# A decoder block with expert retrieval: row gathers through four buffers, tied to their blocks, and dense tiles normed one by one

## The chip, the cores and the metric

The kernel runs on one core of a Trainium2 chip. The metric is the device time in microseconds of one execution. TensorE (PE) multiplies matrices, VectorE (DVE), ScalarE (ACT) and GpSimd (POOL) work on tiles, and SyncE (SP) issues transfers. Each engine takes its instructions in the order in which they stand in its queue: an instruction that waits holds up all that stand behind it.

## The reference

A block of a decoder over 1024 tokens and 16 meta tokens (width 1024): a convolution branch and an RWKV-7 branch side by side, gated and mixed, then a channel mixer that looks up experts (PEER), then a norm. This study turns on the channel mixer and the norm:

```python
s = jnp.einsum('thcd,hcnd->thcn', q, sub_keys)          # 8 heads, 2 x 128 keys
...                                                     # top 16 of each, top 16 of the sums
e = (i1 * PEER_NKEYS + i2).reshape(TOK_BLOCK, PEER_HEADS * K)     # 128 experts per token
gate = jax.nn.softmax(best_s, axis=-1).reshape(TOK_BLOCK, PEER_HEADS * K)
u = expert_u[e]
act = jax.nn.gelu(jnp.einsum('td,ted->te', xb, u), approximate=False)
coef = (gate * act.astype(jnp.float32)).astype(xb.dtype)
return jnp.einsum('te,ted->td', coef, expert_v[e])
...
h = h + peer_ffn(rmsnorm(h, g_ffn[l]), ...)
return rmsnorm(h, g_final)[:, N_META:]
```

There are 16384 experts, 128 blocks of 128. Each expert has a row of 1024 in `expert_u` and one in `expert_v`.

## The kernel before

The 1024 tokens are eight tiles of 128, in two halves. The convolution, the recurrence, the mixing and the routing run for half 0 and then for half 1. The channel mixer is done in two ways at once.

**Three tiles (0, 1, 2) by gathering.** `gather_rows` is a generator. For each of 128 places `j` of a tile it takes a buffer `row` (128 x 2048, 8 KB per partition, `NROW` = 3 of them), issues on GpSimd an indirect DMA (L1005) that fetches for each token the rows u and v of its j-th expert from `euv`, 1 MB in all, multiplies on VectorE the u half with the token's input and sums (L1008, "the product"), takes Gelu and the gate on ScalarE (L1009, L1010), and adds the v half, scaled, to the tile's sum `yr` in PSUM (L1000, "the add"). A buffer is free again after the add. For tile 0 the input `xng` is read from SBUF, for tiles 1 and 2 it is first copied to PSUM (`xr`, L996). When a tile's 128 rows are done, `final` (L1035 on) norms it and stores it. `xng` has two buffers, which the input, the residual `y0` of tiles 1 and 2 and the norm's `sqf` share.

**Five tiles (4 to 7 and 3) densely.** `spread_gates` turns indices and gates into a dense matrix of gates per block of experts. `u_stage` multiplies all 512 tokens of half 1 with the u of one block (24 matmuls of 512 columns) and takes Gelu. For 68 of the 128 blocks (`PRE`) this happens ahead, and the result goes to memory and is read back as `g`. Tile 3's activations come from `gather_coefs`, which gathers u rows alone (L1027) in two runs, before and after place `NEARLY` = 62.

The dense stage is `dense`. It takes groups of `NB` = 4 blocks. For each block it gets the activations, multiplies them with the gates (L1134) and splits the result into a high and a low part, `c2` (L223 on ScalarE, L224 on GpSimd; the profile calls it `c`). Then, for each half `n` of the 1024 columns, it loads the v of the four blocks (`vraw`), splits them likewise (`vhi`, `vlo`), and for each of the five tiles runs 12 matmuls (four blocks, three each: `mm3`, L227 to L229) into one of four PSUM banks, which VectorE adds into the tile's sum (L1161; `hbuf`, `hr` in the profile). After each block it calls the generator for tiles 1 and 2: 8 rows at block 3, then 2 per block, the last at block 127.

In the last group ScalarE squares and sums each finished half of a dense tile (L1164). After the loop, the generator is run out (`for _ in rows`), `g_final` is loaded, the five tiles' sums are normed together (`rstd`: two tiny operations of VectorE, Ln, Exp and Square on ScalarE, two more on VectorE), and each tile is scaled by its factor and by `g_final` and stored. Tiles with even number in the list on VectorE, with odd number by ScalarE (L1174) and GpSimd (L1175).

**Order.** The order of every engine's queue is fixed when the program is built: a list scheduler walks through the instructions with estimated durations, and takes, for each engine, the ready instruction that comes first in the program. Buffers are given out by the same walk. `tc.issue_after(x)` adds that an instruction stands behind `x` on the same engine. It is used before the change for 14 gathers of tile 0 (`pace`). `tc.high_priority(offset=LATER)` puts the gathers of tiles 3 and 0 behind all other work of their stretch. Tile 0 runs beside the mixing, routing and spreading of half 1 and ends shortly after the dense stage has begun, at about 2315 us.

**Tiles of half 1.** Indices and gates of each half are `idx0`, `gate0`, `idx1` and `gate1` (128 x 512 each), made by `residual`. `hist` holds the last columns of the convolution's input from half 0 for half 1, and `carry` the recurrence's state between the halves and then the last output tile of the recurrence.

## Time and profile before

| | us |
|---|---|
| median of three runs | 3659.9 |
| lowest and highest | 3624.96, 3678.22 |
| the profiled execution | 3653.25 |
| its span, first to last instruction | 3651.5 |
| PE busy | 3282.5 (90%) |
| DVE busy | 2684.8 (74%) |
| POOL busy | 2280.4 (62%) |
| ACT busy | 1563.9 (43%) |
| mean granted clock of PE | 0.944 |
| moved by the DMA | 867.66 MB, 238 GB/s |

The profiled execution is one run. Its own time stands beside its span, and what lies around the span is under 2 us. A share of busy time is a mean over stages with different limits; the rows below go by stage. A PE matmul's duration in a row covers its pipeline, so matmuls overlap, and their pace is read from the distance of their starts.

### The profile page before, as it was taken

What the parts mean: (1) busy time and instruction counts of PE and PEld (TensorE: products, weight loads), DVE (VectorE), ACT (ScalarE), POOL (GpSimd) and SP (SyncE); (2) the same over time, 40 slices, a digit from 0 to 9 for tenths busy, and PEclk for the clock granted to TensorE, in tenths of its full rate; (3) what the DMA queues carried; (4) which work ended last, traced back from release to release, by engine and by line L of the source; (5) the groups of instructions that cost most, each with busy time, mean ns of one, the idle gap of its engine ahead of it and who ended that gap; (6) DMA issues with size and microseconds to landing.
All of it is one profiled execution on the core that took longest, in us unless ns stands there. A gap on an engine that the chain in (4) does not pass through costs nothing.

```text
span 3651.5 us, 49244 instructions
## 1 busy us (share of the span) xinstructions
PE 3282.5 (90%) x16175; PEld 2635.6 (72%) x16175; DVE 2684.8 (74%) x5108; ACT 1563.9 (43%) x3714; POOL 2280.4 (62%) x2123
## 2 busy tenths in 40 slices
PE   7999998888788998788899996899999998989994
PEld 7887776677566776676688885777777776777773
DVE  2566538969986775899999887666767666667777
ACT  5555443243444444433367774333333343333333
POOL 3442304535787655656888886676777766767774
PEclk9999979999998899999899998999999999999997
DMA  4321213333677676854699999888889888888987
GB/s 152 113 66 48 60 44 121 107 131 97 199 222 243 180 230 226 308 183 153 215 333 345 351 344 317 285 316 311 319 331 333 332 304 309 319 305 316 329 329 277
DMA packets 347381, 867.66 MB, mean 238 GB/s; under 512 B 53208, under 2 KB 132704, under 8 KB 293876
## 3 DMA queue, kind: packets, MB, share of 16 engines
q0 software_dynamic: 75328, 475.06, 36.0%
q1 hardware_dynamic: 182436, 328.77, 26.9%
q10 hardware_dynamic: 89360, 60.68, 5.4%
q8 instruction: 128, 2.10, 0.2%
q14 instruction: 129, 1.06, 0.1%
HBM read 777.48 MB, written 86.92 MB: 237 GB/s over the span
## 4 chain that ended last, share of the span: by engine, by line
PE 30%; DVE 20%; DMA 13%; issue 10%; POOL 8%; ACT 2%; POOLq 0%; ACTq 0%; DVEq 0%; SPq 0%
DMA row<-euv,idx 6%; PE zp L227 5%; PE zp L229 5%; PE zp L228 5%; PE py L227 3%; PE pg L1088 3%; PE py L228 3%; PE py L229 3%; POOL vlo L224 2%; DVE row L1008 2%; DMA gd<-gt 2%; DVE yr L1000 2%; DVE cy L348 2%; DMA vraw<-euv 2%; POOL row L1027 2%
## 5 line engine op out<-in xcount | busy, mean ns | idle before, releaser
L1005 POOL DMA_INDIRECT row<-euv,idx x384 | 411.2, 1071 | 319.6 <-DVE yr L1000 231.9
L1000 DVE SCALAR_TENSOR_TENSOR yr<-row,act,yr 128x1024 f32<-128x1024 f32 x384 | 493.2, 1284 | 153.9 <-ACT act L1010 151.6
L1008 DVE SCALAR_TENSOR_TENSOR row<-row,xr 128x1024 f32<-128x1024 f32 x256 | 311.5, 1217 | 164.4 <-DMA row<-euv,idx 157.5
L224 POOL TENSOR_TENSOR vlo<-vraw,vhi 128x512 fp32r<-128x512 f32 x256 | 330.8, 1303 | 156.7 <-ACT vhi L223 139.9
L224 POOL TENSOR_TENSOR ul<-ur,uh 128x512 fp32r<-128x512 f32 x256 | 340.3, 1336 | 38.6 <-ACT uh L223 32.2
L1009 ACT ACTIVATE act<-act 128x1 f32<-128x1 f32 x384 | 76.7, 200 | 644.2 <-DVE row L1008 635.3
L227 PE MATMUL py<-vhi,c 128*128 128x512 f32 x640 | 259.0, 409 | 75.8 <-DVE hbuf L1161 32.6
L227 PE MATMUL zp<-x,uh 128*128 128x512 f32 x784 | 315.5, 402 | 7.9 <-ACT g L1101 7.9
L229 PE MATMUL zp<-x,ul 128*128 128x512 f32 x784 | 314.4, 401 | 6.3 <-POOL ul L224 6.3
L228 PE MATMUL zp<-x,uh 128*128 128x512 f32 x784 | 314.4, 401 | 0.0
L229 PE MATMUL py<-vhi,c 128*128 128x512 f32 x640 | 255.6, 406 | 17.0 <-POOL c L224 16.7
L227 PE MATMUL zp<-vhi,c 128*128 128x512 f32 x640 | 251.4, 401 | 21.4 <-DVE hbuf L1161 15.2
L223 ACT ACTIVATE vhi<-vraw 128x512 fp32r<-128x512 f32 x256 | 159.9, 626 | 255.7 <-DMA vraw<-euv 129.4
L228 PE MATMUL py<-vlo,c 128*128 128x512 f32 x640 | 257.1, 402 | 0.4 <-POOL vlo L224 0.4
L228 PE MATMUL zp<-vlo,c 128*128 128x512 f32 x640 | 251.8, 398 | 0.0
L229 PE MATMUL zp<-vhi,c 128*128 128x512 f32 x640 | 249.3, 398 | 0.0
L348 DVE SCALAR_TENSOR_TENSOR cy<-u,vec,cy 128x512 f32<-128x512 f32 x240 | 243.4, 1014 | 5.4
L1008 DVE SCALAR_TENSOR_TENSOR row<-row,xng 128x1024 f32<-128x1024 f32 x128 | 217.4, 1700 | 14.3 <-DMA row<-euv,idx 14.3
L1029 DVE SCALAR_TENSOR_TENSOR row<-row,xng 128x1024 f32<-128x1024 f32 x128 | 184.5, 1447 | 57.4 <-DMA row<-euv,twice 57.1
L1027 POOL DMA_INDIRECT row<-euv,twice x128 | 152.7, 1193 | 111.7 <-DVE row L1029 73.0
L227 PEld LDWEIGHTS py<-vhi,c 128*128 128x128 f32 x640 | 124.3, 194 | 118.6 <-DVE hbuf L1161 43.3
L223 ACT ACTIVATE uh<-ur 128x512 fp32r<-128x512 f32 x256 | 159.3, 625 | 98.6 <-PE zp L228 51.0
(1666 smaller groups left out, 9267.7 us busy)
## 6 DMA issues: line engine op xcount, KB each, us to landing
vraw<-euv SPq DMA_DIRECT2D x256, 256.0 KB, 6.0
ur<-eut SPq DMA_DIRECT2D x256, 256.0 KB, 6.0
gd<-gt ACTq DMA_DIRECT2D x20, 1920.0 KB, 20.8
gblk<-gd SPq DMA_DIRECT2D x30, 1280.0 KB, 11.4
gs<-g SPq DMA_DIRECT2D x68, 256.0 KB, 7.1
g<-gs SPq DMA_DIRECT2D x68, 256.0 KB, 5.9
wbr<-w_in SPq DMA_DIRECT2D x64, 256.0 KB, 3.0
wqr<-w_q SPq DMA_DIRECT2D x64, 256.0 KB, 3.4
```

Of the source, the lines that this page charges most:

```text
L223: A.activation(hi, src, AF.Copy)
L224: return eng.tensor_sub(lo, src, hi.bitcast(F32))
L227: PE.matmul(ps, whi, xhi, start=first, stop=False)
L228: PE.matmul(ps, whi, xlo, start=False, stop=False)
L229: PE.matmul(ps, wlo, xhi, start=False, stop=last)
L348: V.scalar_tensor_tensor(y, u[:, j:j + 512], cw, y, op0=OP.mult, op1=OP.add)
L1000: V.scalar_tensor_tensor(y, row[:, 1], act[:, j:j + 1], y, op0=OP.mult, op1=OP.add)
L1005: G.indirect_dma_start(out=row.rearrange("p a d -> p (a d)"), out_offset=None, in_=a["euv"], in_offset=bass.IndirectOffsetOnAxis(ap=idx[0] ...
L1008: V.scalar_tensor_tensor(row[:, 0], row[:, 0], 1.0, xn, op0=OP.mult, op1=OP.mult, accum_out=aj)
L1027: G.indirect_dma_start(out=row, out_offset=None, in_=a["euv"].rearrange("e (k d) -> (e k) d", k=2), in_offset=bass.IndirectOffsetOnAxis(ap ...
L1029: V.scalar_tensor_tensor(row, row, 1.0, xn, op0=OP.mult, op1=OP.mult, accum_out=act[:, j:j + 1])
L1088: PE.matmul(pg[:, x], o2[:, x], o1[:, x], start=True, stop=True)
```

## The change

- `NROW` goes from 3 to 4: four row buffers for all gathers of whole rows and for the second run of `gather_coefs`. Its first run stays at three.
- Each gather of tiles 1 and 2 is put, in GpSimd's queue, behind the split of the current block's coefficients (`after[0]`).
- `xng` has one buffer instead of two. The input, the residual, the norm's result and `g_final` take turns in it.
- `idx1` and `gate1` are no tiles of their own any more: they are `hist` (made as wide as they need) and `carry`.
- The 256 rows of tiles 1 and 2 are dealt evenly to blocks 3 to 119: 8 at block 3, then `256 * (b + 1) // 120 - 256 * b // 120`, 2 or 3 per block. Blocks 120 to 127 have none. The generator is run out before the second half of the last group, `tables()` loads the table of Ln and Exp there, and `g_final` is loaded.
- Each dense tile is normed and stored right after its last add in the second half of the last group (`last`), with all multiplications on VectorE.

```diff
@@ -37,8 +37,9 @@
 DT = list(range(4, 8)) + list(range(NGT, 4))
 NG, NQ, GB, NB = WD // GT, 512 // GT, 4, 4
 PRE = [b for b in range(128) if b // 4 % 2 == 0 or b >= 120]
-NROW = 3
+NROW = 4
 NV2 = 6
+NROWS, LAST = (NGT - 1) * P, 120
 SOONER = 300
 PACE0 = 22
 NEARLY = 62
@@ -162,8 +163,8 @@
             h = hp.tile([P, 4, D], F32, name="hbuf1")
             hb1.append(h)
             hb.extend(h[:, t] for t in range(4))
-        idx.append(hp.tile([P, 4, P], I32, name=f"idx{hf}"))
-        gate.append(hp.tile([P, 4, P], F32, name=f"gate{hf}"))
+        idx.append(hist.bitcast(I32) if hf else hp.tile([P, 4, P], I32, name="idx0"))
+        gate.append(carry if hf else hp.tile([P, 4, P], F32, name="gate0"))
         if hf == 0:
             coef.append(hp.tile([P, P], F32, name="coef"))
 
@@ -171,7 +172,7 @@
 
         return pool(top, "hb0r")
     idx, gate, coef = [], [], []
-    hist = cp.tile([P, 4, NCONV - 1], F32, name="hist")
+    hist = cp.tile([P, 4, P], F32, name="hist")
     carry = cp.tile([P, 4, P], F32, name="carry")
     si = [0] * 4
     def tables():
@@ -978,13 +979,13 @@
         return x2
 
 
-    def gather_rows(gp, tiles, nrow, pace, yp, rp=None):
+    def gather_rows(gp, tiles, nrow, pace, yp, rp=None, after=()):
 
         for tt in tiles:
-            xn = gp.tile([P, D], F32, name="xng", bufs=2)
+            xn = gp.tile([P, D], F32, name="xng")
             G.dma_start(xn, xg[tt])
             act = gp.tile([P, P], F32, name="act")
-            y0 = gp.tile([P, D], F32, name="y0", tag="hr0" if rp is None else "xng", bufs=1 if rp is None else 2)
+            y0 = gp.tile([P, D], F32, name="y0", tag="hr0" if rp is None else "xng")
             G.dma_start(y0, hd[tt])
             y = hb[tt] = yp.tile([P, D], F32, name="yr")
             moves = [(y, y0)]
@@ -1001,7 +1002,7 @@
 
             for j in range(P):
                 row = gp.tile([P, 2, D], F32, name="row", bufs=nrow)
-                with tc.issue_after(pace[j]) if j in pace else ExitStack():
+                with tc.issue_after(after[0]) if after else tc.issue_after(pace[j]) if j in pace else ExitStack():
                     G.indirect_dma_start(out=row.rearrange("p a d -> p (a d)"), out_offset=None, in_=a["euv"],
                                          in_offset=bass.IndirectOffsetOnAxis(ap=idx[0][:, tt, j:j + 1], axis=0))
                 aj = act[:, j:j + 1]
@@ -1017,13 +1018,13 @@
 
     def gather_coefs(gp, tt, j0, j1):
 
-        xn = gp.tile([P, D], F32, name="xng", bufs=1 + (j1 == P))
+        xn = gp.tile([P, D], F32, name="xng")
         G.dma_start(xn, xg[tt])
         act = coef[0]
         twice = gp.tile([P, j1 - j0], I32, name="twice")
         V.tensor_single_scalar(twice, idx[0][:, tt, j0:j1], 1, op=OP.logical_shift_left)
         for j in range(j0, j1):
-            row = gp.tile([P, D], F32, name="row", bufs=NROW)
+            row = gp.tile([P, D], F32, name="row", bufs=NROW if j1 == P else 3)
             G.indirect_dma_start(out=row, out_offset=None, in_=a["euv"].rearrange("e (k d) -> (e k) d", k=2),
                                  in_offset=bass.IndirectOffsetOnAxis(ap=twice[:, j - j0:j - j0 + 1], axis=0))
             V.scalar_tensor_tensor(row, row, 1.0, xn, op0=OP.mult, op1=OP.mult, accum_out=act[:, j:j + 1])
@@ -1034,7 +1035,7 @@
     def final(sp, tt, nrow):
         y = hb[tt]
         ss = sp.tile([P, 1], F32, name="ssf")
-        q = sp.tile([P, D], F32, name="sqf", tag="xng", bufs=2)
+        q = sp.tile([P, D], F32, name="sqf", tag="xng")
         A.activation(q, y, AF.Square, accum_out=ss)
         r = rstd(sp, ss, 1, 1.0 / D, 1e-6, "rf")
         gq = sp.tile([P, 2, D], F32, name="gq", tag="row", bufs=nrow)[:, 0]
@@ -1104,7 +1105,8 @@
     def dense(es, x2, gp, hr, direct, gk1, vr, yp):
 
         cb = pool(es, "cb")
-        rows = gather_rows(gp, range(1, NGT), NROW, {}, yp, pool(es, "rp", 1, PSUM))
+        after = [None]
+        rows = gather_rows(gp, range(1, NGT), NROW, {}, yp, pool(es, "rp", 1, PSUM), after)
         vb = pool(es, "vb", 2, side="right")
         gk = [hr, gk1]
         yps = pool(es, "yps", 2, PSUM)
@@ -1116,6 +1118,14 @@
 
         gtile = None
         ss = cb.tile([P, 2, NDT], F32, name="ssd")
+        def last(t, tt):
+
+            V.tensor_add(ss[:, 0, t:t + 1], ss[:, 0, t:t + 1], ss[:, 1, t:t + 1])
+            r = rstd(cb, ss[:, 0, t:t + 1], 1, 1.0 / D, 1e-6, f"rd{t % 2}")
+            q = cb.tile([P, D], F32, name="yo", tag="c2", bufs=NB + 1)
+            V.scalar_tensor_tensor(q, hb[tt], r, gf, op0=OP.mult, op1=OP.mult)
+            (A if t % 2 else SY).dma_start(out[tt * P:(tt + 1) * P], q)
+
         for g0 in range(0, P, NB):
             blks = range(g0, g0 + NB)
             cs = []
@@ -1133,7 +1143,7 @@
                     act = u_stage(b, None, x2, bank())
                 V.tensor_mul(g1.rearrange("p (q t) -> p q t", q=NQ), act.rearrange("p (q t) -> p q t", q=NQ), gtile[:, :NQ, b % GB])
                 c2 = cb.tile([P, 2, WD], F32R, name="c2", bufs=NB + 1)
-                split(c2[:, 0, :512], c2[:, 1, :512], g1)
+                after[0] = split(c2[:, 0, :512], c2[:, 1, :512], g1).ins
                 split(c2[:, 0, 512:].rearrange("p (q t) -> p q t", t=GT), c2[:, 1, 512:].rearrange("p (q t) -> p q t", t=GT),
                       gtile[:, NQ:, b % GB])
                 cs.append(c2)
@@ -1141,7 +1151,7 @@
                     for tt in range(NGT, 4):
                         hb[tt] = gp.tile([P, D], F32, name="hr3", tag="hr0")
                         SY.dma_start(hb[tt], hd[tt])
-                for _ in range(0 if b < NB - 1 else 2 * NB if b == NB - 1 else 2):
+                for _ in range(0 if b < NB - 1 else NROWS * (b + 1) // LAST - (NROWS * b // LAST if b >= NB else 0)):
                     next(rows, None)
             for n in range(2):
                 ns = slice(512 * n, 512 * n + 512)
@@ -1153,6 +1163,12 @@
                     lo = vb.tile([P, 512], F32R, name="vlo", bufs=NV2)
                     split(hi, lo, raw)
                     vs.append((hi, lo))
+                if n and g0 == P - NB:
+                    for _ in rows:
+                        pass
+                    tables()
+                    gf = gp.tile([P, D], F32, name="gf", tag="xng")
+                    SY.dma_start(gf, a["g_fin"].to_broadcast([P, D]))
                 for t, tt in enumerate(DT):
                     tsl = slice(t * P, t * P + P)
                     ys = bank()
@@ -1162,20 +1178,8 @@
                     if g0 == P - NB:
                         q = gk[t % 2].tile([P, 512], F32, name="sq", tag="gblk")
                         A.activation(q, hb[tt][:, ns], AF.Square, accum_out=ss[:, n, t:t + 1])
-        for _ in rows:
-            pass
-        gf = cb.tile([P, D], F32, name="gf", tag="c2", bufs=NB + 1)
-        SY.dma_start(gf, a["g_fin"].to_broadcast([P, D]))
-        V.tensor_add(ss[:, 0], ss[:, 0], ss[:, 1])
-        r = rstd(cb, ss[:, 0], NDT, 1.0 / D, 1e-6, "rd")
-        for t, tt in enumerate(DT):
-            q = cb.tile([P, D], F32, name="yo", tag="c2", bufs=NB + 1)
-            if t % 2:
-                A.activation(hb[tt], hb[tt], AF.Copy, scale=r[:, t:t + 1])
-                G.tensor_mul(q, hb[tt], gf)
-            else:
-                V.scalar_tensor_tensor(q, hb[tt], r[:, t:t + 1], gf, op0=OP.mult, op1=OP.mult)
-            (A if t % 2 else SY).dma_start(out[tt * P:(tt + 1) * P], q)
+                        if n:
+                            last(t, tt)
 
     def convolution(hf, es, z, between):
         cv = pool(es, f"cc{hf}", side="right")
```

Left out of the diff are the two lines that read and write `hist`, which now name its first 30 columns.

## Rows read from the trace of the kernel before

**Rows 1.** Windows: stretch, length, busy us PE PEld DVE ACT POOL, clock, DMA share, GB/s
```profile
1850.00:2255.00 405.00, 376.86 (x2237) 329.31 (x2235) 353.45 (x639) 284.80 (x759) 333.16 (x303) 0.98 0.99 342
...
2255.00:3602.00 1347.00, 1252.18 (x5276) 1003.29 (x5276) 938.39 (x1227) 485.89 (x1238) 949.63 (x884) 0.97 0.87 316
...
3602.00:3652.00 50.00, 0.47 (x3) 0.04 (x1) 30.19 (x41) 16.08 (x36) 13.27 (x10) 0.53 0.67 249
```

**Rows 2.** Waits of PE, 2255 to 3602: total us, times, longest us
```profile
PE py L227 <- DVE hbuf L1161: 32.6, 16, 6.5
...
PE py L227 <- ACT c L223: 23.0, 13, 3.6
...
PE py L229 <- POOL c L224: 16.7, 11, 2.5
...
PE zp L227 <- DVE hbuf L1161: 15.2, 8, 4.8
```

**Rows 3.** Timeline of one stall: start us, us; in brackets idle before and releaser
```profile
3034.15 0.96 POOL L1005 DMA_INDIRECT row<-euv,idx  x1 [0.16 <-DMA vraw<-euv]
...
3044.76 1.22 DVE L1008 SCALAR_TENSOR_TENSOR row<-row,xr 128x1024 f32<-128x1024 f32 x1 [8.16 <-DMA row<-euv,idx]
...
3045.90 0.68 DVE L1161 TENSOR_TENSOR hbuf<-hbuf,py 128x512 f32<-128x512 f32 x1
...
3046.64 0.79 PE L227 MATMUL py<-vhi,c 128*128 128x512 f32 x1 [6.48 <-DVE hbuf L1161]
...
3047.23 0.63 PE L228 MATMUL py<-vlo,c 128*128 128x512 f32 x1
...
3051.50 0.63 PE L229 MATMUL py<-vhi,c 128*128 128x512 f32 x1
```

**Rows 4.** Waits of DVE and POOL, 2255 to 3602, same columns
```profile
DVE row L1008 <- DMA row<-euv,idx: 153.9, 95, 8.2
...
POOL row L1005 <- DVE yr L1000: 161.0, 75, 7.2
```

**Rows 5.** The gathers (L1005), 2330 to 3500: their starts, and landing
```profile
L1005 POOL DMA_INDIRECT row<-euv,idx x222: 935/961/1440, 2344.7 to 3495.1; - x111
...
DMA to landing us min/median/max: 5.4/8.1/13.0
```

**Rows 6.** Timeline of the end: last group's matmuls, the last tiles' norms
```profile
3593.15 0.39 PE L227 MATMUL zp<-vhi,c 128*128 128x512 f32 x1
...
3602.07 0.40 PE L229 MATMUL py<-vhi,c 128*128 128x512 f32 x1
...
3602.70 0.68 DVE L1161 TENSOR_TENSOR hr<-hr,py 128x512 f32<-128x512 f32 x1
...
3603.41 0.63 ACT L1164 ACTIVATE sq<-hr 128x512 f32<-128x512 f32 x1 [1.26 <-DVE hr L1161]
...
3640.22 1.29 DVE L1000 SCALAR_TENSOR_TENSOR yr<-row,act,yr 128x1024 f32<-128x1024 f32 x1 [0.60 <-ACT act L1010]
...
3641.54 1.02 ACT L1038 ACTIVATE sqf<-yr 128x1024 f32<-128x1024 f32 x1 [1.35 <-DVE yr L1000]
...
3642.67 1.28 ACT L201 ACT_TABLE_LOAD   x1
...
3647.66 0.33 SPq L1043 DMA_DIRECT2D out<-sqf  x1
```

**Rows 7.** Tile 1 to 2: timeline, then DMA issues (KB, us to landing)
```profile
3000.99 1.28 DVE L1042 SCALAR_TENSOR_TENSOR sqf<-yr,rfr,gq 128x1024 f32<-128x1024 f32 x1
...
3005.10 1.24 ACT L996 ACTIVATE xr<-xng 128x512 f32<-128x512 f32 x2 [0.62 <-DMA xng<-xg]
...
out<-sqf SPq DMA_DIRECT2D x2, 512.0 KB, 4.9
...
xng<-xg POOLq DMA_DIRECT2D x2, 512.0 KB, 8.2
...
y<-hd POOLq DMA_DIRECT2D x2, 512.0 KB, 8.1
```

More of the change, by code (lines that the diff above doesn't have):

```diff
@@ L332, in convolved @@
         else:
-            V.tensor_copy(u[:, :H], hist[:, ct])
+            V.tensor_copy(u[:, :H], hist[:, ct, :H])
         for t0, n, ps in zmain(hi, lo):
@@ L340, in convolved @@
         if off:
-            G.tensor_copy(hist[:, ct], u[:, 512:])
+            G.tensor_copy(hist[:, ct, :H], u[:, 512:])
         y = cv.tile([P, 512], F32, name="cy", bufs=4)
```

## The prediction

> **What bounds the kernel now.** I read the windows by stage first, then TensorE's waits in the dense stage, then one of its stalls in the timeline, then the last 50 us, and last the gathers and the DMA. The windows [rows 1] show a program that is TensorE's until 3602 us: in the 1347 us of the dense stage PE is busy 1252 us at a granted clock of 0.97, DVE 938 us, POOL 950 us. After that come 50 us in which PE does nothing and DVE, the busiest engine, works 30. So there are two places to gain: the tail, and what keeps the dense stage above its floor. The floor: two matmuls of the last group, 40 apart with both ends counted, start 3593.15 and 3602.07, so 39 steps of 0.229 us [rows 6]; 5280 matmuls (32 groups x 2 halves x 5 tiles x 4 blocks x 3, and 60 blocks x 24) take 1208 us at that pace. The stage takes 1347.
>
> What lies between is waiting. PE waits 47.8 us for VectorE's adds into the dense accumulators (32.6 + 15.2, 24 times), and 39.7 us for the coefficients (23.0 + 16.7) [rows 2]. A wait costs more than itself: at 3046.64 PE resumes after 6.48 us, and the matmuls from 3047.23 to 3051.50 start 0.43 us apart (10 steps), the lower of the two clock levels in pace, before the 0.229 returns [rows 3]. Twelve matmuls at 0.2 us more are 2.4 us, 37% on top of the gap. The same rows show why VectorE was late: its queue is in order, and a row's product (L1008) stood at its head for 8.16 us until the gather issued at 3034.15 had landed; the add that PE needed (L1161) came right behind it at 3045.90. Over the stage these products wait 153.9 us for their rows, 95 times, and GpSimd waits 161.0 us, 75 times, for a row buffer to come free (yr L1000) before it can issue a gather [rows 4], with the splits of the next weights queued behind.
>
> The gathers are near the limit of three buffers. 222 of them start between 2344.7 and 3495.1, one per 5.2 us, and land in 8.1 us (median) [rows 5]. A buffer is held from the issue to the end of the row's add: at least 8.1 + 1.2 (product) + 0.6 (two activations) + 1.3 (add) = 11.2 us [rows 3, 5, 6], and at one row per 5.2 us with three buffers at most 15.6. That is why rows are still to come when PE stops: the last add ends at 3641.5 [rows 6].
>
> **The change part by part.** All terms are set against the profiled execution, 3653.25 us (span 3651.5); the median of the three runs, 3659.9, is 6.7 above it.
>
> 1. The tail: the rows dealt to 120 blocks, dense tiles normed one by one. The last matmul ends 3602.47 and the span 3651.5, 49.0 us. With rows dealt so that the last belongs to block 119, two whole groups of four blocks follow, each about 10.5 us per block (1347 / 128), 84 us: the rows and the norm of tile 2 are done before PE is. Then what follows the last matmul is the last dense tile alone. Its add starts 0.23 us after it and its square 0.71 later (3602.70, 3603.41), so 0.94 us to the square. From the start of a square to the end, the last gathered tile needs 3641.54 to 3651.5, 9.96 us, with two table loads of 1.28 us on the way [rows 6]. The changed tail has the table loaded before (the explicit load stands ahead of the last five tiles), a square half as long (-0.4) and one tiny add of the two halves (+0.3, an estimate from its neighbours): 9.96 - 2.56 - 0.4 + 0.3 = 7.3, and with 0.94 it is 8.2 us. Gain 40.8. VectorE may stand behind one more tile's multiplication (1.28 us and its small operations), so 36 to 41; I take **-40**. The four earlier tiles' norms lie beside the last tiles' matmuls (12 x 0.229 = 2.7 us a tile against 0.7 + 1.3 us and five tiny operations on VectorE, with no row left in its queue). If that cover is gone, because VectorE waits for ScalarE's chain with the next add behind it, each of the four costs at most that chain, some 2 us; the four accumulator banks cover most of it.
>
> 2. Four buffers, each gather behind its block's coefficients. No work is added: 256 gathers, products and adds as before. With four buffers a row may hold its buffer 4 x 4.8 = 19 us instead of 15.6, so GpSimd's 161 us of waits should mostly go. What PE gets of it is bounded by its own waits for the accumulators: all gone is 47.8 x 1.37 = 65 us. But the product is still queued on VectorE by the order written at build time, and one more buffer does not bring a single row sooner; only rows issued in bunches share one wait. On the other side the tie bunches gathers behind the coefficients of the blocks whose activations were computed earlier, which come within a few us of each other, and up to four gathers are then in the DMA at once instead of three. If a landing grew by 4/3, to 10.8, the 95 waits would grow by 2.7 us each, 257 us; of VectorE's 153.9 us, 47.8 reached PE (0.31), so 80 us, and with the slow matmuls 109. Ends -65 and +109; the nearest rows are the present waits, which a mild relief fits better than either end. I take **-12**, a fifth of the gain.
>
> 3. Denser rows and the last two groups without any. 256 rows in 120 blocks are 6.7% more per block: on 65 us of row-made stalls +4. Two of 32 groups free of them: 2/32 x 65 = -4. **0**, bounds -8 and +8.
>
> 4. One buffer instead of two for the gathered tile's input, the residual and the norm's output. At the change from tile 1 to tile 2 the norm's product starts 3000.99 and takes 1.28, and the next tile's input, loaded meanwhile in the other buffer, is copied to PSUM from 3005.10, 1.24 us [rows 7]. With one buffer the load has to wait for the store: 3002.3 + 4.9 (store) + 8.2 (load) [rows 7] + 1.24 = 3016.6 instead of 3006.3, 10.3 us later, and the residual comes after that copy, 8.1 us further on. This stops the row stream twice (tile 0 to 1, 1 to 2). GpSimd issues these loads in order, so the splits behind a waiting load stand too, and VectorE's first product stands with the dense adds behind it. Nothing of it if the order puts other work there, 2 x 10.3 x 1.37 = 28 us if all reaches PE; **+6**, a fifth.
>
> 5. Indices and gates of half 1 in the tiles of the convolution's history and the state: no instruction more, and both tiles are read for the last time before routing writes them. 0. The coefficient gathers and tile 0, before 2255, also get four buffers and the single input buffer; PE is busy 377 of the 405 us from 1850 on with the DMA at 0.99 [rows 1], so there is no room that a buffer could open. 0, with 15 either way (one stop of 10.3 as in part 4, or as much relief).
>
> Sum: -40 - 12 + 0 + 6 + 0 = -46, 3653 - 46 = **3607 us**. Against the median of the runs that would be 1.4% less.
>
> **The rivals.**
> A: the stalls for the accumulators collapse. Then part 2 is -65: 3653 - 40 - 65 + 6 = 3554. For it: the worst waits behind rows come singly, after a buffer came free late. Against it: the 95 waits are spread over the whole stage, and most follow a gather that itself was issued without a wait.
> B, slower than before: the DMA fills up. Place: between the first dense rows and block 119. Now 316 GB/s at a share of 0.87, while the stretch before shows 342 at 0.99 [rows 1]. A row of 1.05 MB per 5.2 us is 201 GB/s, the rest 115. Dealt to 116 blocks of about 10.3 us, 248 rows come one per 4.8 us, 218 GB/s, in all 333, 0.97 of the 342. Landings then stretch, products stand longer at VectorE's head, and part 2 is its upper end: 3653 - 40 + 109 + 6 = 3728. It decides from landings near 10 us; it exceeds the gain as soon as a third of the 109 is real. For it: the demand. Against it: in the stretch at 0.99 PE lost little.
> The Trainium skill, page "DMA: Bandwidth & Descriptors", section "Where 436 GB/s comes from", puts the limit of a core's reads from HBM at about 358 GB/s, which would make the same demand 0.93 and this rival weaker; the trace's 342 at a share of 0.99 is lower and decides, so I keep the chance that follows from 0.97.
> C: the change does not free the tail. If the tie and the stops of part 4 push rows behind block 127 after all, the 49 us stay: 3653 - 12 + 6 = 3647. Against it: 84 us of slack, 17 rows at 4.8 us.
>
> **How the numbers follow.** Forecast 0.50 (its own range 3580 to 3640), A 0.20, B 0.18, C 0.12. A measurement of this kernel tells about 2% from no change: below 3587 or above 3733 against the median. Faster by over 2%: A and a fifth of the forecast, 0.30. Slower: the upper part of B, 0.07. Within: 0.63. The range 3553 to 3690 holds the forecast, C, half of B and the near half of A.
>
> **What would show it.** Part 1: no gather and no L1000 after PE's last matmul, under 11 us from there to the end, no table load there. Part 2: GpSimd's wait for yr well under 161 us, PE's wait for the accumulators somewhat under 48, dense stage 1330 to 1345. Part 4: a pause of about 20 us between the last product of tile 1 and the first of tile 2, with a wait of GpSimd on a store. B would show as landings over 10 us, a DMA share above 0.95 and PE's waits above 100 us; A as a dense stage below 1290. The prediction is wrong if rows remain in the tail or if the dense stage moves by more than 40 us either way.

## The result and the profile after

The changed kernel is slower by 1.0%: median 3689.0 us of 17 runs against 3656.8 us of 17 runs of the kernel before, ratio 1.010 with an interval of [1.008, 1.012]. That is less than 2%, but outside what repetition gives. Forecast were 3607 us, with 3553 to 3690 as the range. The profiled execution took 3689.27 us, its span 3687.3.

The lines of `gather_rows` and all behind it up to the dense stage are one further down: the gather is L1006, the product L1009, the add L1001, the splits L224 and L225, the matmuls L228 to L230, the dense add L1177, the multiplication with the gates L1144.

Windows of the changed kernel (columns as in [rows 1]): the stretch ahead of the dense stage, the pause at its start, its part up to 3560 and the rest with the last rows (until 3614), and the tail.

```profile
1850.00:2253.00 403.00, 387.38 (x2275) 337.63 (x2275) 369.78 (x660) 285.52 (x770) 340.35 (x304) 0.99 0.99 340
2253.00:2289.00 36.00, 5.44 (x24) 4.23 (x23) 17.46 (x22) 8.91 (x26) 12.79 (x11) 0.61 0.74 264
2289.00:3560.00 1271.00, 1173.30 (x4831) 919.02 (x4831) 870.69 (x1149) 444.73 (x1142) 875.36 (x826) 0.97 0.85 320
3560.00:3673.00 113.00, 107.03 (x450) 84.84 (x449) 59.60 (x86) 44.02 (x105) 62.55 (x58) 0.98 0.48 173
3673.00:3688.00 15.00, 0.00 (x0) 0.00 (x0) 7.13 (x17) 2.55 (x11) 0.00 (x0) 0.65 0.41 171
```

The tail of 49.0 us is down to 14.4, as was meant. But the dense stage begins 36 us later (2289 against 2253 for the first matmul with `vhi`) and takes 1384 us instead of 1349. Its waits, from 2289 to 3673, for PE, DVE and POOL:

```profile
PE py L228 <- ACT c L224: 49.8, 12, 30.6
PE zp L228 <- DVE hbuf L1177: 32.6, 17, 5.0
PE zp L229 <- POOL vlo L225: 15.2, 11, 2.1
PE py L228 <- DVE hbuf L1177: 11.9, 7, 3.6
PE py L229 <- POOL vlo L225: 9.7, 9, 2.0
...
PE py L228 <- DVE hr L1177: 3.6, 5, 1.2
...
DVE row L1009 <- DMA row<-euv,idx: 108.7, 67, 6.7
DVE g L1144 <- DMA g<-gs: 60.3, 17, 9.8
...
POOL row L1006 <- DVE yr L1001: 165.7, 51, 9.9
```

Against [rows 2, 4]: VectorE's waits for rows fell from 153.9 us to 108.7. But TensorE's waits for the accumulators are 48.1 (32.6 + 11.9 + 3.6) where they were 47.8, GpSimd's waits for a row buffer are 165.7 where they were 161.0, and TensorE now also waits for `vlo` (15.2 + 9.7, before 0.4). Of the first line's 49.8 us, 30.6 are the pause ahead of the first matmul with `vhi`, where the kernel before stands 19.9 us. The fourth buffer moved the waits; it did not take them away. TensorE's second longest wait for an accumulator shows what an add can now stand behind: a multiplication with the gates that had waited 9.84 us for its load.

```profile
2976.78 0.69 DVE L1144 TENSOR_TENSOR g<-g,gblk 128x512 f32<-128x512 f32 x1 [9.84 <-DMA g<-gs]
2977.39 0.68 DVE L1177 TENSOR_TENSOR hbuf<-hbuf,zp 128x512 f32<-128x512 f32 x1
...
2978.12 0.79 PE L228 MATMUL zp<-vhi,c 128*128 128x512 f32 x1 [4.08 <-DVE hbuf L1177]
```

A row lands somewhat later than in [rows 5]; the gathers of 2330 to 3500:

```profile
L1006 POOL DMA_INDIRECT row<-euv,idx x232: 932/957/1422, 2330.0 to 3496.3; - x116
...
DMA to landing us min/median/max: 5.3/9.1/13.7
```

The end, where [rows 6] showed rows until 3641:

```profile
3612.28 1.28 DVE L1001 SCALAR_TENSOR_TENSOR yr<-row,act,yr 128x1024 f32<-128x1024 f32 x1
...
3663.36 0.40 PE L228 MATMUL zp<-vhi,c 128*128 128x512 f32 x1
...
3672.46 0.40 PE L230 MATMUL py<-vhi,c 128*128 128x512 f32 x1
3672.89 0.69 DVE L1177 TENSOR_TENSOR hr<-hr,py 128x512 f32<-128x512 f32 x1 [0.85 <-PE py L230]
3673.62 0.63 ACT L1180 ACTIVATE sq<-hr 128x512 f32<-128x512 f32 x1 [0.94 <-DVE hr L1177]
3673.88 1.28 DVE L1126 SCALAR_TENSOR_TENSOR yo<-hbuf,rd1r,gf 128x1024 f32<-128x1024 f32 x1
3676.77 1.28 DVE L1126 SCALAR_TENSOR_TENSOR yo<-hbuf,rd0r,gf 128x1024 f32<-128x1024 f32 x1
3678.09 0.20 ACT L202 ACTIVATE rd1r<-rd1m 128x1 f32<-128x1 f32 x1 [1.82 <-DVE yo L1126]
3679.26 1.28 DVE L1126 SCALAR_TENSOR_TENSOR yo<-hbuf,rd1r,gf 128x1024 f32<-128x1024 f32 x1
3682.15 1.28 DVE L1126 SCALAR_TENSOR_TENSOR yo<-hr,rd0r,gf 128x1024 f32<-128x1024 f32 x1
```

The last add of a row ends at 3614, 59 us ahead of TensorE. What is left are four norms in a row, 2.5 to 2.9 us each, because each one's ScalarE operations start only when VectorE is done with the tile before.

**The account**, by three marks in the timeline: the last matmul of half 1's gate matrix (`wbh`), the first and the last matmul with `vhi`.

| us | before | after | difference |
|---|---|---|---|
| start to the last `wbh` | 1152 | 1136 | -16 |
| `wbh` to the dense stage | 1101 | 1153 | +52 |
| dense stage | 1349 | 1384 | +35 |
| tail | 49.0 | 14.4 | -35 |
| span | 3651.5 | 3687.3 | +36 |

The -16 is no gain: TensorE's queues of the two programs are the same up to about 1240 us, and the runs of the kernel before alone lie between 3620 and 3683 us. So a single profile says little about 16 us of total time; medians decide, and profiles serve to see where time lies. Dense stage and tail together take 1398 us before and after: the dense stage lost what the tail gained, and what makes the changed kernel slower in the profile is the 52 us ahead of it.

### The profile page after: what moved, and what is told of

Read it like the earlier page. It is cut to its first block, busy times and chain, and to the rows that moved or that the text cites. A ratio compares the mean times of both kernels' runs of the same rounds, so it can differ in the third digit from the quotient of the medians.

```text
span 3687.3 us, 49184 instructions
## 1 busy us (share of the span) xinstructions
PE 3325.1 (90%) x16175; PEld 2645.2 (72%) x16175; DVE 2671.3 (72%) x5126; ACT 1558.4 (42%) x3724; POOL 2282.1 (62%) x2121
## 5 line engine op out<-in xcount | busy, mean ns | idle before, releaser
L1006 POOL DMA_INDIRECT row<-euv,idx x384 | 414.0, 1078 | 311.3 <-DVE yr L1001 206.4
L1001 DVE SCALAR_TENSOR_TENSOR yr<-row,act,yr 128x1024 f32<-128x1024 f32 x384 | 493.1, 1284 | 132.8 <-ACT act L1011 130.8
L225 POOL TENSOR_TENSOR ul<-ur,uh 128x512 fp32r<-128x512 f32 x256 | 337.1, 1324 | 113.3 <-ACT uh L224 107.0
L1009 DVE SCALAR_TENSOR_TENSOR row<-row,xr 128x1024 f32<-128x1024 f32 x256 | 310.7, 1215 | 110.2 <-DMA row<-euv,idx 108.7
L225 POOL TENSOR_TENSOR vlo<-vraw,vhi 128x512 fp32r<-128x512 f32 x256 | 327.4, 1298 | 78.6 <-ACT vhi L224 75.9
L230 PE MATMUL zp<-x,ul 128*128 128x512 f32 x784 | 313.1, 400 | 8.7 <-POOL ul L225 8.7
L228 PE MATMUL zp<-x,uh 128*128 128x512 f32 x784 | 314.4, 401 | 4.7 <-ACT g L1102 4.3
L228 PE MATMUL py<-vhi,c 128*128 128x512 f32 x640 | 256.7, 409 | 66.3 <-ACT c L224 49.8
L228 PE MATMUL zp<-vhi,c 128*128 128x512 f32 x640 | 255.0, 411 | 34.9 <-DVE hbuf L1177 32.6
L229 PE MATMUL zp<-vlo,c 128*128 128x512 f32 x640 | 260.3, 409 | 15.3 <-POOL vlo L225 15.2
L230 PE MATMUL py<-vhi,c 128*128 128x512 f32 x640 | 252.9, 403 | 5.4 <-POOL c L225 5.4
L230 PE MATMUL zp<-vhi,c 128*128 128x512 f32 x640 | 254.9, 406 | 2.3 <-POOL c L225 2.3
L224 ACT ACTIVATE vhi<-vraw 128x512 fp32r<-128x512 f32 x256 | 157.7, 623 | 160.9 <-DMA vraw<-euv 61.5
L1030 DVE SCALAR_TENSOR_TENSOR row<-row,xng 128x1024 f32<-128x1024 f32 x128 | 183.9, 1445 | 56.0 <-DMA row<-euv,twice 55.4
L224 ACT ACTIVATE uh<-ur 128x512 fp32r<-128x512 f32 x256 | 159.8, 626 | 148.1 <-PE zp L229 78.0
L225 POOL TENSOR_TENSOR c<-g,c 128x512 fp32r<-128x512 f32 x128 | 165.9, 1296 | 73.9 <-ACT c L224 73.3
L1009 DVE SCALAR_TENSOR_TENSOR row<-row,xng 128x1024 f32<-128x1024 f32 x128 | 204.7, 1603 | 1.3 <-DMA row<-euv,idx 1.3
```

Of the source, the lines that this page charges most:

```text
L224: A.activation(hi, src, AF.Copy)
L225: return eng.tensor_sub(lo, src, hi.bitcast(F32))
L228: PE.matmul(ps, whi, xhi, start=first, stop=False)
L229: PE.matmul(ps, whi, xlo, start=False, stop=False)
L230: PE.matmul(ps, wlo, xhi, start=False, stop=last)
L1001: V.scalar_tensor_tensor(y, row[:, 1], act[:, j:j + 1], y, op0=OP.mult, op1=OP.add)
```

## The experiments

Theory after the result: the loss has two places, the fourth buffer in the coefficient gathers and tile 0 (ahead of the dense stage), and the dense stage itself. Rivals: the tie, the single input buffer, and the move of tiles in SBUF: `hist` grew from 480 bytes a partition to 2048, so that the tiles behind it, the coefficients `c2` among them, moved by an odd multiple of 32 bytes.

All runs in one table: from the profiles the stretch from `wbh` to the dense stage, the dense stage, and the tail, in us; then the median, and its ratio to the kernel before on the same chip with the interval. e5, e6 and e9 to e12 have the pad of e1. The stretches come from one execution each, and it need not be a typical one: e6's took 3603 us where its median is 3624, e12's 3628 where its median is 3616. e8 has the queues of the kernel before, and its stretch to the dense stage is 15 us longer; smaller differences in that column mean nothing.

| run | to dense | dense | tail | median | ratio |
|---|---|---|---|---|---|
| before | 1101 | 1349 | 49 | 3656.8 | |
| after | 1153 | 1384 | 14 | 3689.0 | 1.010 [1.008, 1.012] |
| e1 after, addresses as before | 1149 | 1368 | 14 | 3685.0 | 1.011 [1.006, 1.015] |
| e2 after, no tie | 1158 | 1374 | 14 | 3677.4 | 1.007 [1.004, 1.010] |
| e3 after, three buffers | 1087 | 1342 | 92 | 3674.1 | 1.004 [1.001, 1.007] |
| e4 before, one input buffer | 1119 | 1337 | 65 | 3659.4 | 1.001 [0.998, 1.003] |
| e5 fourth buffer in the dense stage alone | 1088 | 1400 | 14 | 3646.0 | 1.001 [0.998, 1.004] |
| e6 the same, no tie | 1081 | 1381 | 14 | 3623.9 | 0.995 [0.992, 0.998] |
| e7 before, dealing and tail alone | 1113 | 1346 | 66 | 3668.6 | 1.007 [1.004, 1.010] |
| e8 before, addresses moved by 32 bytes | 1116 | 1349 | 49 | 3659.4 | 1.003 [1.000, 1.006] |
| e9 fourth buffer from tile 0 on | 1151 | 1399 | 14 | 3702.5 | 1.013 [1.007, 1.019] |
| e10 fourth for coefficients and dense | 1129 | 1387 | 14 | 3675.7 | 1.007 [1.003, 1.010] |
| e11 e5 dealt to 126 blocks | 1089 | 1398 | 17 | 3653.1 | 1.001 [0.997, 1.004] |
| e12 e6, gate product on GpSimd | 1095 | 1363 | 15 | 3615.9 | 0.991 [0.990, 0.993] |

**e1, the addresses put back.**

```diff
     carry = cp.tile([P, 4, P], F32, name="carry")
+    cp.tile([P, 8], F32, name="pad")
```

> The changed kernel with 32 bytes of padding behind carry: every engine's queue is the same, instruction for instruction; only the coefficients c2 start at a multiple of 64 bytes again, as in the kernel before (36864 there, 38432 in the changed kernel, 38464 here). Theory 'address': the dense matmuls come 0.2291 us apart in the kernel before and 0.2334 in the changed one because their stationary tiles c2 lie at an odd multiple of 32 bytes; then the pace returns to 0.229, the dense stage gets some 16 us shorter (3840 x 0.0042) and the time goes to about 3673. Rival 'pressure': the slower pace comes from the row traffic or the clock; then pace and time stay (3689).

The queues of all engines are those of the changed kernel. The matmuls with `vhi` and `vlo` (3840 in the dense stage) start 0.2275 us apart instead of 0.2333, the dense stage is 16 us shorter in the profile, about what 3840 steps of 0.004 to 0.006 us are worth (15 to 22). The 3673 that the theory gave did not come: the median is 4 us lower and its interval covers that of the changed kernel. So the pace is shown, a gain in time is not, and the stretch ahead of the dense stage stays at 1149.

**e2, no tie.**

```diff
-        rows = gather_rows(gp, range(1, NGT), NROW, {}, yp, pool(es, "rp", 1, PSUM), after)
+        rows = gather_rows(gp, range(1, NGT), NROW, {}, yp, pool(es, "rp", 1, PSUM))
```

> The changed kernel without the tie of the gathers to their blocks' coefficients; all before the dense stage is the same. Theory 'tie': bunched gathers cost the dense stage its stalls and 10 to 20 us of the time come back (about 3672). Rival: with four buffers and the dealing the gathers run ahead of their blocks without the tie, crowd the start of the dense stage, and the time is the same or up to 20 us worse (3689 to 3709).

Without the tie the last row's add ends at 3555 instead of 3614, and the ratio is 1.007 instead of 1.010, with intervals that overlap (12 us between the medians): the theory's direction, but not clear of noise. The tie is not what the tail needs. The stretch ahead is as long as before this edit.

**e3, three buffers.**

```diff
-NROW = 4
+NROW = 3
```

> The changed kernel with three row buffers. Theory 'late rows': with three buffers the rows cannot keep the pace that 120 blocks ask for, gathers run past the last block and a tail of 25 to 45 us comes back: 3710 to 3735 if nothing else changes. Rival 'four buffers only reorder': the fourth buffer is worth nothing in the dense stage, the tail shrinks all the same, and the time is 3689 or lower.

Theory and rival were each half right: the rows are late again, as the one said, but the time is lower than the changed kernel's, as the other said. The one edit takes 66 us from the stretch ahead of the dense stage (1153 to 1087) and 42 from the dense stage, which leaves some of its rows to the tail. The rows come late (last add 3634, TensorE ends at 3578), and the tail is 92 us: 35 us of it after the last add, since the dense norms and tile 2's own now come together there. VectorE waits 151.4 us for rows and GpSimd 156.5 us for buffers, the numbers of the kernel before.

**e4, one input buffer in the kernel before** (`bufs=2` taken from all uses of `xng`).

> The kernel before with one buffer instead of two for the gathered tile's input, residual and norm result (tag xng), and nothing else. Theory 'one input buffer': it is this part that changes the order in the recurrence of half 1 (the first instruction on GpSimd that differs between the two kernels is the load of tile 0's input) and delays tile 0 and the start of the dense stage: 15 to 35 us slower (3672 to 3692). Rival: its cost is only two pauses of 10 us in the row stream, hidden for the most part: 0 to 10 us (3657 to 3667).

No difference that can be measured, as the rival said. The pauses of the row stream are there, though: from the last product of a tile to the first of the next 26.9 and 24.7 us, where the kernel before has 16.5 and 13.5.

**e5 and e6, the fourth buffer in the dense stage alone**, with the pad of e1; e6 without the tie.

```diff
-NROW = 4
+NROW = 3
...
-                row = gp.tile([P, 2, D], F32, name="row", bufs=nrow)
+                row = r4.tile([P, 2, D], F32, name="row4") if r4 and j % 4 == 3 else gp.tile([P, 2, D], F32, name="row", bufs=nrow)
...
-        rows = gather_rows(gp, range(1, NGT), NROW, {}, yp, pool(es, "rp", 1, PSUM), after)
+        rows = gather_rows(gp, range(1, NGT), NROW, {}, yp, pool(es, "rp", 1, PSUM), after, pool(es, "r4"))
```

> The changed kernel with three row buffers for the coefficient gathers and tile 0 and a fourth one, from a pool of its own opened in the dense stage, that takes every fourth row of tiles 1 and 2; and with the 32 bytes of padding. Up to the dense stage every queue is that of the run with three row buffers, in the dense stage the rows have four as in the changed kernel. Theory 'early stages': what the changed kernel loses, it loses before the dense stage (its four buffers in the recurrence and mixing of half 1: the dense stage begins 1153 us after the last gate matmul of half 1 instead of 1101 in the kernel before and 1087 with three buffers) and by the address of c2; then the dense stage begins near 2235, takes 1350 to 1370, and the tail is 14: 3605 to 3625, faster than both kernels. Rival 'dense': the fourth buffer with the tie and the dealing makes the dense stage itself slow, and the time stays above 3650.

> The same without the tie of the gathers; all before the dense stage is the same. Theory 'tie costs': in the changed kernel the dense stage was some 10 us shorter without the tie (1374 against 1384) and its rows were done 59 us earlier; then this run is 5 to 15 us faster than the one with the tie. Rival: that was one profile against another, and the two are equal within 5 us.

The stretch ahead is 1088 and 1081 us and the tail 14: the loss ahead of the dense stage is gone, the gain behind it is kept. e5's 3646 lies between what the theory and the rival gave for it, since its dense stage came out as the rival said. The tie costs 22 us between the two medians, with the same queues up to the dense stage and intervals apart, more than the 5 to 15 expected. e6 is the first version that beats the kernel before, by 0.5%. But their dense stages, 1400 and 1381 us, are among the longest of the table, although rows are waited for far less. e5's waits from 2230 to 3630:

```profile
PE zp L229 <- DVE hbuf L1178: 29.9, 23, 4.3
PE py L229 <- DVE hr L1178: 22.4, 9, 5.9
...
DVE row L1010 <- DMA row<-euv,idx: 54.7, 36, 3.9
...
POOL row L1007 <- DVE yr L1002: 225.5, 87, 8.8
```

VectorE waits 54.7 us for rows (153.9 in [rows 4]), GpSimd 225.5 for buffers (161.0), and TensorE's waits for the adds of VectorE are not less (61.7 with `hr`, against 47.8). One of the three stalls of 5.9 us, in the timeline:

```profile
2501.69 0.94 POOL L1007 DMA_INDIRECT row<-euv,idx  x1 [6.58 <-DVE yr L1002]
2504.71 0.94 POOL L1007 DMA_INDIRECT row<-euv,idx  x1 [2.09 <-DVE yr L1002]
2505.67 1.30 POOL L226 TENSOR_TENSOR c<-g,c 128x512 fp32r<-128x512 f32 x1
2506.92 0.86 POOL L226 TENSOR_TENSOR c<-gblk,c 128x128 fp32r<-128x128 f32 x2
2507.74 3.69 POOL L226 TENSOR_TENSOR vlo<-vraw,vhi 128x512 fp32r<-128x512 f32 x3
...
2506.09 5.89 DVE L1145 TENSOR_TENSOR g<-g,gblk 128x512 f32<-128x512 f32 x1
2511.91 0.67 DVE L1178 TENSOR_TENSOR hr<-hr,py 128x512 f32<-128x512 f32 x1
...
2512.63 0.80 PE L229 MATMUL py<-vhi,c 128*128 128x512 f32 x1 [5.89 <-DVE hr L1178]
```

GpSimd stands 6.58 us for a buffer, with the splits queued behind. Then it works through six of them without a pause, until 2511.43. VectorE's multiplication of two tiles in SBUF, started beside the first, ends at 2511.98, after 5.89 us instead of 0.69, and the add that TensorE needs stands behind it. It is no wait in the views; it shows as an operation that is too long. Of the 68 such multiplications in e5, the 30 with no split beside them take at most 0.71 us, the 38 others 1.95 on average; the 60 that read PSUM, 54 of them beside a split, never take over 0.70. The changed kernel is not slowed by this: there the 68 take 0.95 us on average, in the kernel before 0.96, in e5 1.40 and in e6 1.19. The Trainium skill, page "SBUF — State Buffer", section "Who interferes with whom", says that a VectorE instruction with two inputs in SBUF contends with a GpSimd instruction that reads SBUF; the trace agrees, and shows that a whole row of GpSimd's operations can pass first.

**e7, the dealing and the tail alone, in the kernel before** (three buffers, two input buffers, no tie; `LAST`, `last` and the run-out as in the change).

> The kernel before with only the new dealing of the rows and the norm of each dense tile on its own, with its three row buffers and two input buffers. The order of every queue is that of the kernel before up to the last group. Theory 'late rows': with three buffers the rows are late whatever blocks they are dealt to, and the norms of the dense tiles, now behind the last row, come on top: the tail grows from 49 to 80 or 95 us and the time to 3685 to 3705. Rival, the prediction's term of the tail: the dealing alone frees the tail, and the time falls by 40 us to 3613.

The queues are those of the kernel before up to the last group: with three buffers the rows come when a buffer is free, not when the loop asks for them. So dealing them to 120 blocks brings nothing forward, the norms wait behind the rows, the tail grows to 66 us, less than the 80 to 95 of the theory, and the time to 3669. It takes the fourth buffer to free the tail; a fourth buffer with the old dealing was not run.

**e8, the kernel before with its tiles moved by 32 bytes** (the pad, without the rest).

> The kernel before with 32 bytes of padding: every queue is the same, c2 starts at an odd multiple of 32 bytes (36896 for 36864). Theory 'address': the dense matmuls come 0.2333 us apart instead of 0.2291 and, 3840 of them, cost 16 us: 3669. Rival: address has no part in it: 3653 and 0.229.

The pace goes from 0.2291 to 0.2333 us as in the changed kernel, with the same queues. But the dense stage is 1349 us in both: as TensorE runs slower it waits less, 79 us within the stage instead of 93. The median is 10 us higher, the interval touches 1. So the address sets the pace; that it costs time is not shown.

**e9 and e10: coefficients or tile 0.** Both take e5 and add the fourth buffer ahead of the dense stage, once for tile 0's rows, once for the second run of the coefficient gathers.

```diff
-                row = r4.tile([P, 2, D], F32, name="row4") if r4 and j % 4 == 3 else gp.tile([P, 2, D], F32, name="row", bufs=nrow)
+                row = gp.tile([P, 2, D], F32, name="row4") if j % 4 == 3 else gp.tile([P, 2, D], F32, name="row", bufs=nrow)
```

> The kernel of e5 (three buffers for the second run of the coefficient gathers, with the pad that restores the old addresses of the coefficient tiles), but the fourth buffer is there for the rows of tile 0 as well as in the dense stage; the tie stays. Theory: the 50 us that were lost between the end of half 1's gate matrices and the dense stage come from the coefficient gathers with four buffers, because their products on VectorE fall between the operations of the recurrence. Then that stretch stays at 1085 to 1105 us as in e5 (1088) and the median at 3640 to 3660. Rival: the loss comes from tile 0's rows (1.05 MB each, against 0.5 MB) on four buffers. Then the stretch is 1135 to 1160 and the median 3680 to 3705.

In e10 tile 0 keeps three buffers (`if after and j % 4 == 3`), and the coefficients have:

```diff
-            row = gp.tile([P, D], F32, name="row", bufs=NROW if j1 == P else 3)
+            row = gp.tile([P, D], F32, name="row4") if j1 == P and j % 4 == 3 else gp.tile([P, D], F32, name="row", bufs=3)
```

> The mirror of e9: four buffers for the second run of the coefficient gathers, three for tile 0, four in the dense stage, pad and tie. By the theory the stretch from the end of half 1's gate matrices to the dense stage is 1135 to 1160 us as in the changed kernel (1153) and the median 3680 to 3705; by the rival 1085 to 1105 us and 3640 to 3660. If both halves of the cause count, each of e9 and e10 shows 1110 to 1130 and 3660 to 3680.

The theory that named the coefficients alone falls. Either is enough: tile 0's rows cost 63 us there (1088 to 1151; ratio 1.013 against 1.001), as the rival said, the coefficients 41 (ratio 1.007). Where it is lost shows when the starts of like matmuls are lined up with the last `wbh`. Against the kernel before, after 316 us the changed kernel is 46 us late, e9 38, e10 39, but e5 8 and e3 1 us. That is the recurrence of half 1. It is not all. Against e3, which has three buffers and the rest of the change, the changed kernel, e9 and e10 are still 40, 35 and 43 us late 960 us after `wbh`, but 66, 64 and 42 when the dense stage begins: where tile 0 has four buffers, some 25 us more go in the last 100 us, beside its last rows. TensorE's pause there, ahead of the first matmul with `vhi`, is 30.6 us in the changed kernel and 30.7 in e9, against 14.6 in e10, 13.0 in e3 and 19.9 in the kernel before.

The recurrence first. In its second 100 us after `wbh`, before, changed, e10, e9, e3:

```profile
1252.00:1352.00 100.00, 97.91 (x686) 76.43 (x685) 74.02 (x134) 41.05 (x110) 60.09 (x76) 0.96 0.71 211
```

```profile
1236.00:1336.00 100.00, 89.37 (x474) 67.49 (x474) 67.33 (x121) 28.67 (x78) 63.60 (x75) 0.74 0.67 209
```

```profile
1232.00:1332.00 100.00, 85.89 (x476) 64.89 (x475) 68.55 (x123) 29.57 (x80) 64.30 (x75) 0.76 0.67 213
```

```profile
1238.00:1338.00 100.00, 92.58 (x578) 70.38 (x577) 66.25 (x117) 35.98 (x96) 56.37 (x71) 0.86 0.62 191
```

```profile
1248.00:1348.00 100.00, 95.43 (x610) 72.64 (x610) 67.07 (x124) 37.87 (x102) 61.89 (x73) 0.88 0.64 202
```

With the fourth buffer TensorE gets through 474 to 578 matmuls where it did 610 to 686, at a granted clock of 0.74 to 0.86. Its busy share hardly shows it, because slower matmuls are also busy. What these rows don't bear out is that more rows crowd VectorE: in these 100 us the coefficient products take 48 us of VectorE in the kernel before, 46 in the changed one, 47 in e10 and 44 in e9 and e3. Nor is it the traffic of tile 0's rows: in e9 a single one of their gathers starts before 231 us after `wbh`, and 21 us against e3 are lost by 200. What does differ is the order: a free buffer makes a gather ready earlier in the scheduler's estimate, and from there TensorE and VectorE take the recurrence's operations in another order. Three-buffer kernels with other orders lie between 1081 and 1119, four-buffer ones between 1129 and 1158. Which operation in the new order holds up the recurrence, and what part the lower clock has in it as cause or as consequence, was not tested; nor was what lengthens the pause at the end.

**e11, e5 dealt to 126 blocks.**

```diff
-NROWS, LAST = (NGT - 1) * P, 120
+NROWS, LAST = (NGT - 1) * P, 126
```

> e5 with the rows dealt to 126 blocks instead of 120, so that each block has 5% fewer. Two theories of what four buffers and the tie cost in the dense stage. Density: a pair of groups takes 88 to 95 us with 18 to 20 rows and 85.5 with 16, so fewer rows per block shorten the dense stage of e5 (1400) to 1375 to 1390, with the last row's add some 40 us later (near 3610) and still ahead of TensorE's end; median 3625 to 3638. Place: the tie itself, which puts a gather behind a split that is late, costs the time however the rows are dealt; the dense stage stays at 1395 to 1405 and the median at 3640 to 3655.

Dense stage 1398, median 3653.1 with 3653.4 for the kernel before: how dense the rows are dealt is not what costs. That leaves the tie, whose 22 us e6 shows. (Without the tie the number of blocks does not matter at all: e6 with 126 has the same queues as with 120, and was not run.)

**e12, the gate product on GpSimd.**

```diff
-                V.tensor_mul(g1.rearrange("p (q t) -> p q t", q=NQ), act.rearrange("p (q t) -> p q t", q=NQ), gtile[:, :NQ, b % GB])
+                (G if b in PRE else V).tensor_mul(g1.rearrange("p (q t) -> p q t", q=NQ), act.rearrange("p (q t) -> p q t", q=NQ), gtile[:, :NQ, b % GB])
```

> e6 with one engine changed: the product of the activations read back from memory with their gates (g<-g,gblk, 68 blocks, both operands in SBUF) is done by GpSimd instead of VectorE. In e6's trace this product takes 0.69 us where no GpSimd tensor operation runs beside it and up to 5.89 us where GpSimd works through a row of splits, and three of TensorE's longest stalls (18.6 us) end with it. Theory: those stalls go with the contention. Then no operation of VectorE in the dense stage but the row work is over 1.3 us, the stalls of 6 us are gone, the dense stage falls from 1381 to 1350 to 1365 and the median from 3624 to 3595 to 3610. Rival: GpSimd gets 68 x 1.3 = 88 us more work and becomes late itself, so that TensorE's waits for vlo and c (32.6 us in e6) grow by as much or more; dense stage 1380 to 1410, median 3620 to 3655.

The dense stage is 1363 us, 18 less than e6's, within what the theory gave; the median is 3615.9, 30 us under the kernel before on the same chip (0.9%) and some 6 above the theory's band. Against e6, whose interval overlaps, the 8 us between the medians are not clear of noise. TensorE's waits from 2240 to 3640:

```profile
PE py L229 <- ACT c L225: 57.4, 15, 12.7
PE py L231 <- POOL c L226: 25.8, 12, 8.4
PE zp L229 <- DVE hbuf L1178: 15.5, 7, 4.3
PE py L229 <- DVE hbuf L1178: 5.7, 4, 2.6
```

The waits for the accumulators are 21.2 us, where the kernel before had 47.8 and e6 48.7. Waits for `c` on ScalarE grew from 45.0 to 57.4 us; those for GpSimd's `c` and `vlo` did not grow. No wait for an add is over 4.3 us any more, where e6 had two of 5.9. This version has the lowest median of the study: four buffers in the dense stage alone, the new tail, no tie, and the product off VectorE.

## Why the prediction was wrong

The sign was wrong: -46 forecast, +36 in the profile and +32 in the medians. By its own steps:

1. **The tail, -40: right, a little too large.** 49.0 to 14.4 us is -35, with no row, no gather and no table load behind the last matmul. The 8.2 us left out that the norms would bunch: "what follows the last matmul is the last dense tile alone" failed. Three norms still stood ahead of that tile's, 2.5 to 2.9 us each: the case of the lost cover, which had been priced at some 2 us a tile. And the means was mistaken: dealing the rows to 120 blocks frees nothing by itself (e7, e3); it takes the fourth buffer.
2. **Four buffers and the tie, -12: wrong sign.** "GpSimd's 161 us of waits should mostly go" failed: 165.7 in the changed kernel, 225.5 in e5. GpSimd runs ahead until the buffers are full, with four as with three; the fourth lets it run further ahead and then wait as long. The relief for VectorE came (153.9 to 108.7, in e5 to 54.7), but not to TensorE: in place of adds late behind rows came adds late behind gate products that waited for their loads, as at 2976.78 above, and late `vlo`; in e5 and e6 gate products beside GpSimd's splits. The fifth of the gain that was taken had no mechanism behind it. The dense stage is 35 us longer, inside the ends of -65 and +109; up to 16 of it may be the slower pace (e1), though e8 has that pace and no longer stage. The tie costs 22 us (e5 against e6); e2's 12 are not clear of noise.
3. **Denser rows, 0:** not seen apart; e11 agrees.
4. **One input buffer, +6: not contradicted.** The pauses grew by 10.4 and 11.2 us in e4 (26.9 - 16.5, 24.7 - 13.5), where 10.3 was worked out; e4's ratio allows anything from -6 to +11 us. In the changed kernel they are 29.1 and 36.1 us, and GpSimd's wait on the store is there (1.08 us at 2967.92).
5. **Dead tiles and the early stages, 0 with 15 either way: this is the step that failed.** "There is no room that a buffer could open" was argued from the windows from 1850 on [rows 1], and they do not change (clock 0.99, DMA 340 GB/s). But the fourth buffer is given out from about 1150 us on, beside the recurrence, which no row of the prediction looked at. Ahead of the dense stage it costs 41 to 66 us (e10 and e9 against e5, the change against e3), some 40 of them in the recurrence and, with tile 0, some 25 in the last 100 us. That the fourth buffer does this is shown; through which operation is open. And the dead tiles were no pure renaming: the wider `hist` moved the coefficient tiles to addresses at which the matmuls go at 0.2333 us instead of 0.2291.

The rivals: B (the DMA fills up) had the right sign and the wrong cause: landings of 9.1 us, a DMA share of 0.85 in the stretch with rows, no more than before. C fell, since the tail was freed; A fell, since the waits for the accumulators went from 47.8 to 48.1 us. Neither of the prediction's two signs of being wrong came, no row is left in the tail and the dense stage moved by less than 40 us: it had set no sign for the stage in which the time was lost. The measured median lies at the upper edge of the range, held by B's half, not by a cause that had been seen.

## What to carry to other kernels

One more buffer in a shared constant changes every stage that uses the constant, and where a scheduler fixes the queues it changes their order: look at the profile of each of these stages, not only of the one that is meant, and give the buffer to that one alone (e5 has a ratio of 1.001 where the changed kernel with the same addresses, e1, has 1.011). A producer that waits for buffers can wait as long with one more (161.0 us before, 165.7 after); what counts is whether its consumer's lateness reached the bound engine. And when a wait vanishes without a gain, look for operations that have become longer, since contention between engines shows in durations and not in the views of waits.

## What was not expected of the hardware

VectorE's 128x512 multiplication with both inputs in SBUF, 0.69 us by itself, took up to 5.89 us beside a row of GpSimd's tensor operations, and ended just after them; with one input in PSUM it never did (60 of 60 at 0.70 us or less). And the pace of 512-column matmuls depends on where the tiles lie: with the coefficient tiles at a multiple of 64 bytes (36864) they start 0.2291 us apart, at an odd multiple of 32 (36896) 0.2333, with the same queues (e8). The other pair goes the same way, 38432 with 0.2333 and 38464 with 0.2275 (e1); why the two multiples of 64 differ is open. In the fence of the end above, 39 steps from 3663.36 to 3672.46 are 0.2333 each, where [rows 6] had 0.229. Through the dense stage the granted clock is 0.97 in both kernels; the u stage's matmuls stay at 0.2268 us. That the address is the cause rests on e1 and e8, which changed nothing else; why it matters is open, and so is whether it costs time, since e8's dense stage was no longer for it.
